# A 32-expert layer on one core: another order of the expert groups, 26 weight units, host-made layouts, and a gate that moves out of the front

## The chip, the cores and the metric

One core of a Trainium2 chip (trn2). The metric is the time of one execution on the device in microseconds (us); lower is better. Host-side preparation of the inputs is outside it. A difference is given in us or in per cent of the median before.

## The reference, cut to what matters

`x` has 256 tokens of 1024 features, `ctx` another 256. All is float32.

```python
sh1, sc1, g1, sh2, sc2, g2 = ada_params(c, ada_w, ada_b)     # silu(c) @ ada_w + ada_b, six parts of 1024
hx = modulate(x, sh1, sc1)                                    # layer norm, then *(1+sc1) + sh1
proj_x = hx @ w_in                                            # q, k, v and the 2*512 columns of the gating unit
att_x = neighbourhood_attention(q_x, k_x, v_x, k_c, v_c, rpb) # 8 heads, window and context keys in one softmax
sgu_x = spatial_gating(gelu(proj_x[..., U_OFF:]), ...)        # 128x128 mixing matrix for each of 4 groups
x = layer_norm(ALPHA * x + g1 * (concat(att_x, sgu_x) @ w_out), ln1_g, ln1_b)
h = modulate(x, sh2, sc2)
gates = softmax of the 4 largest of h @ router_w + router_b   # 32 experts
for e in range(32):                                           # w_gu: 1024x2048, w_down: 1024x1024
    gu = h @ w_gu[e] + b_gu[e]
    y += gate[e] * (((clip(gu[1024:]) + 1) * swiglu(gu[:1024])) @ w_down[e] + b_down[e])
x = layer_norm(ALPHA * x + g2 * y, ln2_g, ln2_b)
```

## The kernel before, in words

**The front** computes the adaLN vectors, the projection, attention, gating, the output projection, the first layer norm and the router. **The experts** follow: all 32 are computed, each with 12 MB of weights, cut into 12 pieces of 1 MB (8 of `w_gu`, 4 of `w_down`).

**The ring.** SBUF holds `NU` = 24 units of 8 KB per partition. `unit` takes the first of the list `free_slots`, `release` puts one at its end. Everything large lives in units: the weights of the front, working tiles, the expert pieces. The list is worked out when the program is written: a DMA into a unit waits, on the chip, for the last instruction that uses what lay there before, wherever in the program that instruction stands. `stream` is the list of all pieces in the order in which they are wanted; `pump` takes a unit and issues the next piece, `weights` hands out a piece, `done` releases its unit and pumps one more, unless that would leave fewer than `reserve[0]` free. Nearly all DMAs are issued in this one order by SyncE (SP), with eight in flight at most, and SP issues nothing past one that waits.

**The groups.** Experts are ranked by token count on the chip, so several share the 128 rows of a matmul: a *quad* is four experts of 32 rows (48 pieces), a *pair* two of 64 rows (24 pieces), a *single* one of 128 rows (12 pieces). Group 0 is the experts 0 and 1; twelve groups follow in the order of `PLAN`. Each goes through `group`: `gu_step` for gate half 0, linear half 0, gate half 1, linear half 1, each with a hook between its two halves of the contraction (`in0` to `in3`), `swiglu_gate` and `swiglu_lin` on VectorE (DVE) and ScalarE (ACT), `h_T`, then `down`, `scaled`, and the `scatter` of the group before at `gu1`.

**What the steps touch.** `front_u` is one unit for the whole front: silu(c) (`sT`, the stationary operand of every ada step), the router's weights, the ada biases. It is released (L1010) just before group 0. `ada_step` (L605) multiplies one 1 MB block of `ada_w`; the four blocks `adaG` give the second residual's gate g2. Two run as fillers of the attention, two inside `route_mm(0)` (L901), then `finish_G` (L849) spreads g2 over the partitions on GpSimd (POOL). `flip_heads` (L350) and `mask_bias` (L527) make the table of position biases on PE, ACT and POOL. `spread` (L1401) makes the rows ln2_g and ln2_b into 128 partitions. `overflow_items` (L1322) is a loop under a condition on a count, for experts with more tokens than their rows; its body does not run here, but SP waits there for every DMA in flight. `down_cols` is used in the last group only, with small last pieces (`DOWN_ROWS`).

```python
PLAN = [QUADS[0], SINGLES[0], PAIRS[0], QUADS[1], PAIRS[1], SINGLES[1], QUADS[2], PAIRS[2], PAIRS[3], QUADS[3], PAIRS[4],
        PAIRS[5]]
...
    def done(key, refill=True):
        release(loaded.pop(key)[0])
        if refill:
            pump(1, keep=reserve[0])
...
        if gi == 5:
            l2_u, row_u = unit("l2"), unit("row")
            reserve[0] = 0
            SP.dma_start(row_u[0:1, 0:D], ln2_g)
```

Of the kernel before, what the change touches and what calls it, by code (L numbers as in the profile page):

```python
# [9 lines left out]
F32 = mybir.dt.float32  # L10
# [24 lines left out]
PLAN = [QUADS[0], SINGLES[0], PAIRS[0], QUADS[1], PAIRS[1], SINGLES[1], QUADS[2], PAIRS[2], PAIRS[3], QUADS[3], PAIRS[4],  # L35
        PAIRS[5]]
DOWN_ROWS = (((0, 512), (512, 512)), ((0, 512), (512, 256), (768, 128), (896, 128)))
NU = 24


def front_blocks():
# [13 lines left out]
    for name, col in (("adaS", 4096), ("adaG", 5120)):  # L55
        out += [((name, i), "ada_w", i * 256, col, 1024) for i in range(4)]
        if name == "adaS":
            out += wo[0:2]
    return out
# [6 lines left out]
def hybrid_layer_kernel(  # L66
    ctx: ExitStack,
    tc: tile.TileContext,
    x, c, cx, c_ctx, w_front, ada_b, rpb, sgu_ln_g, sgu_ln_b, sgu_w, sgu_b,
# [8 lines left out]
    ada_b, rpb = ada_b[0], rpb[0]  # L78
    sgu_w, sgu_b = sgu_w[0], sgu_b[0]
# [105 lines left out]
    SP.dma_start(crow[0:8, :], c.rearrange("o (k p) -> (o k) p", p=P))  # L185
    SP.dma_start(crow[8:16, :], c_ctx.rearrange("(k p) -> k p", p=P))
# [12 lines left out]
    G.memset(flip, 1.0)  # L199
    G.affine_select(out=flip, in_=flip, compare_op=ALU.is_equal, fill=0.0, base=-63, pattern=[[1, 64]],  # L200
                    channel_multiplier=1)
    G.memset(bsel, 0.0)
    G.memset(bsel[:, :, 0:2], 1.0)
    G.affine_select(out=bsel, in_=bsel, compare_op=ALU.is_equal, fill=0.0, base=0,
                    pattern=[[1, 12], [0, 32]], channel_multiplier=-1)
    one_r = cst.tile([12, 1], F32, name="one_r")
    G.memset(one_r, 0.0)
    for r in (2, 3, 8, 9):
        G.affine_select(out=one_r, in_=one_r, compare_op=ALU.not_equal, fill=1.0, base=-r,
                        pattern=[[0, 1]], channel_multiplier=1)  # L210
# [8 lines left out]
    stream.extend((key, block(i, n)) for i, (key, _, _, _, n) in enumerate(FRONT))  # L219

    def group_stream(gid, ranks, by_cols=False):
# [17 lines left out]
        def col_piece(a, r0, rows, col, n):  # L239
            def fn(t):  # L240
                v = t[:, 0:rows // P * n].rearrange("p (k n) -> p k n", n=n)
                for r in range(r0, r0 + rows, 256):
                    k0, k1 = r // P % 2, min(r // P % 2 + (r0 + rows - r) // P, 2)
                    SP.dma_start(v[:, (r - r0) // P:(r - r0) // P + k1 - k0, :],  # L244
                                 expert(w_dn, a)[r // 256].rearrange("p (k n) -> p k n", k=2)[:, k0:k1, col:col + n])
                return v
            return fn
# [7 lines left out]
        if by_cols:  # L255
            for nn in range(2):
                for r0, rows in DOWN_ROWS[nn]:
                    for a in range(n):
                        stream.append(((gid, "c", nn, r0, a), col_piece(a, r0, rows, nn * 512, 512)))
        else:  # L260
            for i in range(4):
                for a in range(n):
                    stream.append(((gid, "d", i, a), piece(w_dn, a, i, 1024)))

    group_stream(0, None)

# [23 lines left out]
    T2_u = [unit("T2") for _ in range(2)]  # L290
    T2 = [u[:, 0:1536].rearrange("p (h m n) -> p h m n", h=4, m=6) for u in T2_u]
# [28 lines left out]
    def ln_transpose(t):  # L320
        for hh in range(2):
            pt = ax_bank()
            for k in range(4):
# [4 lines left out]
    pT = ax_bank()  # L328
    PE.transpose(pT[:, 0:16], crow, ident[32:48, 32:48])
    sg = front_u[:, 2016:2048].rearrange("p (a n) -> p a n", a=2)  # L330
    S.activation(sg[:, 0, :], pT[:, 0:16], AF.Exp, scale=-1.0)
# [3 lines left out]
                    pT[:, 0:16].rearrange("p (i k) -> p i k", i=2), op=ALU.mult)  # L335


    r0_ = R_u[64:128, 0:64]

    def flip_begin(h, b):  # L340
        for r2 in range(2):
            PE.matmul(b[64 * r2:64 * r2 + 64, 0:384], flip,
                      bass.AP(tensor=r0_.tensor, offset=r0_.offset + h * 250 + (1 - r2) * 31,
                              ap=[list(r0_.ap[0]), [31, 6], [1, 64]]), start=True, stop=True)
        return h, b

    def flip_end(h, b):
        S.copy(T2[h // 4][:, h % 4], b[:, 0:384].rearrange("p (m n) -> p m n", m=6))

    def flip_heads(hs):  # L350
        for h in hs:
            flip_end(*flip_begin(h, ax_bank()))
# [7 lines left out]
    flip_heads(range(0, 1))  # L360
# [3 lines left out]
    flip_heads(range(1, 2))  # L364
# [3 lines left out]
    V.tensor_scalar_add(adab, adab, one_r)  # L368
# [12 lines left out]
    ones_b = cst.tile([P, P], BF16, name="ones_b")  # L381
    G.memset(ones_b, 1.0)
# [6 lines left out]
    fold4 = cst.tile([P, NE], F32, name="fold4")  # L389
# [19 lines left out]
    def ada_quarter(q):  # L409
        bank = ax_bank()  # L410
        for j in range(4):
            row = (2 if j > 1 else 0) + q // 2
            off = (q % 2) * 256 + (j % 2) * P
            PE.matmul(bank[32 * j:32 * j + 32, 0:P], bsel[:, row, :], adab[:, off:off + P],
                      start=True, stop=False)
        for k in range(KT):
            for j in range(4):
                w = weights(("ada", j // 2, q))
                PE.matmul(bank[32 * j:32 * j + 32, 0:P], sT[:, k, :], w[:, k, (j % 2) * P:(j % 2 + 1) * P],
                          start=False, stop=k == KT - 1)  # L420
        for i in range(2):
            done(("ada", i, q))
        rows = rowsq[q % 2]
        V.tensor_copy(rows, bank[:, 0:P])
        return bank, rows
# [80 lines left out]
    fl = [flip_begin(h, ax_bank()) for h in range(2, 4)]  # L506
# [975 lines left out]
```

## Time and profile before

| what | value |
|---|---|
| runs before | 1157.69, 1158.47, 1159.37 us; median 1158.47 us |
| profiled execution | 1159.04 us, of which the span of the trace is 1157.3 us |
| PE busy, granted clock | 1011.2 us (87% of the span), mean clock 0.949 |
| DVE, ACT, POOL busy | 311.0, 137.7, 40.1 us |
| moved by DMA | 449.76 MB, mean 389 GB/s |

The trace is of one execution, 0.57 us above the median; 1.74 us of its time lie outside the span. Times in the rows are us from the span's start. A busy PE is not a PE at its peak, and the idle time of an engine costs something only where the end waits for it.

### The profile page before, as it was taken

To read this page: it belongs to the slowest core of one execution; us is meant where nothing else is said; L and a number is where in the kernel's file an instruction comes from. 1 tells how busy PE (TensorE), PEld (TensorE's weight loads), DVE (VectorE), ACT (ScalarE), POOL (GpSimd) and SP (SyncE) were. 2 spreads that over 40 slices of the span, in tenths; PEclk is the share of its full clock that TensorE was granted. 3 is DMA by queue.
4 is the path that set the end of the run, shared out by engine and by line. 5 is a ranking of instruction groups with operands and counts; after the bars stand their busy time and mean duration, and the time that the engine had idled before them with its cause. 6 is when DMAs were issued, how large, how long until landed. Compare 5 with 4: busy or idle time off the path is not lost. (4 is left out here: it accounts for less than half of the span.)

```text
span 1157.3 us, 13460 instructions
## 1 busy us (share of the span) xinstructions
PE 1011.2 (87%) x5225; PEld 427.9 (37%) x5225; DVE 311.0 (27%) x621; ACT 137.7 (12%) x297; POOL 40.1 (3%) x72
## 2 busy tenths in 40 slices
PE   6999998999779999976759999879999777689995
PEld 4798555443213534221114353213434112124221
DVE  5687756313103121210111212102121111012114
ACT  4344343110000101000001010000101000000000
POOL 3300301000000000000000000000000000000000
PEclk9999998999989999998869999989999989899998
DMA  9977789889999999999998978999999999999985
GB/s 346 372 277 290 303 305 389 301 372 426 426 428 426 427 427 426 427 426 428 427 426 351 427 262 347 425 428 427 427 426 427 427 426 427 427 426 427 426 334 206
DMA packets 68624, 449.76 MB, mean 389 GB/s; under 512 B 8495, under 2 KB 9663, under 8 KB 15565
## 3 DMA queue, kind: packets, MB, share of 16 engines
q1 hardware_dynamic: 68534, 448.85, 94.2%
q8 instruction: 42, 0.69, 0.2%
q14 instruction: 24, 0.20, 0.0%
q10 hardware_dynamic: 24, 0.02, 0.0%
HBM read 447.80 MB, written 1.05 MB: 388 GB/s over the span
## 5 line engine op out<-in xcount | busy, mean ns | idle before, releaser
L1192 PE MATMUL mm<-w,xg 128*32 128x512 f32 (+2 forms) x2048 | 419.2, 616 | 37.2 <-DMA w<-in_exp_w_gu_dram 37.1
L1236 PE MATMUL mm<-w,t 128*32 128x512 f32 (+2 forms) x960 | 226.2, 695 | 54.1 <-DMA w<-in_exp_w_down_dram 45.4
L1192 PEld LDWEIGHTS mm<-w,xg 128*32 128x32 f32 (+2 forms) x2048 | 128.2, 130 | 314.7 <-issue 236.6
L1236 PEld LDWEIGHTS mm<-w,t 128*32 128x32 f32 (+2 forms) x960 | 62.8, 140 | 205.7 <-issue 108.2
L1276 DVE TENSOR_TENSOR t<-mm,late 128x512 f32<-128x512 f32 x26 | 18.0, 692 | 271.2 <-PE mm L1236 256.3
L1215 DVE TENSOR_SCALAR t<-mm 128x512 f32<-128x512 f32 x26 | 18.0, 692 | 244.9 <-PE mm L1192 244.9
L1208 ACT ACTIVATE t<-t 128x512 f32<-128x512 f32 x26 | 16.4, 630 | 519.2 <-DVE t L1206 519.2
L1206 DVE TENSOR_SCALAR t<-mm 128x512 f32<-128x512 f32 x26 | 18.0, 691 | 201.3 <-PE mm L1192 201.3
L972 PE MATMUL mm<-bgu,sel 32*128 32x512 f32 x104 | 58.2, 639 | 1.3 <-DVEq L1324 1.3
L1259 PE MATMUL ax<-t,sT 128*128 128x512 f32 x100 | 46.2, 604 | 0.8 <-DVE t L1276 0.8
L270 POOL TENSOR_TENSOR rs<-rs,mhalf 128x1 f32<-128x1 f32 x12 | 10.0, 836 | 1056.4 <-DVE mv L282 931.6
L1227 ACT COPY t<-ax 128x512 f32<-128x512 f32 x26 | 15.0, 577 | 260.6 <-PE ax L1223 260.6
L966 PE MATMUL ax<-oh,tM 128*128 128x128 f32 x384 | 44.8, 275 | 0.0
L966 PEld LDWEIGHTS ax<-oh,tM 128*128 128x128 f32 x384 | 43.8, 192 | 0.0
L1261 DVE TENSOR_TENSOR xin<-xin,ax 128x512 f32<-128x512 f32 x50 | 33.2, 684 | 5.0 <-PE ax L1259 4.6
L467 DVE TENSOR_TENSOR wlo<-w,whi 128x1024 fp32r<-128x1024 f32 x20 | 30.1, 1540 | 3.5 <-ACT whi L464 3.5
L1259 PEld LDWEIGHTS ax<-t,sT 128*128 128x128 f32 x100 | 18.1, 189 | 28.9 <-issue 23.5
L972 PEld LDWEIGHTS mm<-bgu,sel 32*128 32x128 f32 x104 | 15.3, 183 | 31.7 <-issue 20.4
L858 ACT ACTIVATE xg<-ax,sh,sc 128x128 f32<-128x128 f32 x60 | 22.5, 459 | 32.8 <-PE ax L966 26.8
L1404 PE MATMUL ax<-row,l 1*128 1x512 f32 x8 | 5.7, 851 | 20.5 <-DMA row<-in_ln_g_dram 20.5
L464 ACT CAST whi<-w 128x1024 fp32r<-128x1024 f32 x20 | 20.1, 1049 | 9.4 <-PE mm L499 9.4
L1223 PEld LDWEIGHTS ax<-ident,t 128*128 128x128 f32 x104 | 11.2, 140 | 21.8 <-issue 18.5
(286 smaller groups left out, 788.0 us busy)
## 6 DMA issues: line engine op xcount, KB each, us to landing
w<-in_exp_w_gu_dram SPq DMA_DIRECT2D x256, 1024.0 KB, 19.4
w<-in_exp_w_down_dram SPq DMA_DIRECT2D x120, 1024.0 KB, 19.5
w<-in_w_front_dram SPq DMA_DIRECT2D x38, 1024.0 KB, 7.1
w<-in_exp_w_down_dram SPq DMA_DIRECT2D x14, 512.0 KB, 11.3
xin<-in_x_dram SPq DMA_DIRECT2D x2, 512.0 KB, 3.9
cin<-in_ctx_dram SPq DMA_DIRECT2D x2, 512.0 KB, 8.4
w<-in_exp_w_down_dram SPq DMA_DIRECT2D x4, 256.0 KB, 9.4
out_dram<-xin SPq DMA_DIRECT2D x4, 256.0 KB, 2.0
```

The costliest lines, as they stand in the source:

```text
L464: S.copy(av[:, k], w[:, k])
L467: V.tensor_tensor(bv[:, k], w[:, k], av[:, k].bitcast(F32), op=ALU.subtract)
L858: S.activation(dst[:, kk, :], src, AF.Identity, scale=sc2[:, kk:kk + 1], bias=sh2[:, kk:kk + 1])
L966: PE.matmul(bank[:, k * P:(k + 1) * P], late["tMv"][:, t, (hh * 4 + k) * P:(hh * 4 + k + 1) * P], oh[:, t].rearrange("p n w -> p (n w)"), ...
L972: PE.matmul(b, sel[r, :], bgu[r, :], start=True, stop=False)
L1192: PE.matmul(b[a * w:(a + 1) * w, :], xg[:, half * 4 + k, a * w:(a + 1) * w], weights((gid, part, j, half, a))[:, k, :], start=False, stop= ...
L1206: V.tensor_scalar_min(gtile, b, 7.0)
L1215: V.tensor_scalar(lt, b, 7.0, -7.0, op0=ALU.min, op1=ALU.max)
L1236: PE.matmul(ys[nn][a * w:(a + 1) * w, :], hTt[:, (2 * i + k) * P + a * w:(2 * i + k) * P + (a + 1) * w], weights((gid, "d", 2 * jh + i, a) ...
L1259: PE.matmul(b, st[:, t, :], ys[nn], start=True, stop=True)
L1261: V.tensor_tensor(sl, sl, b, op=ALU.add)
L1276: V.tensor_tensor(y, bank, late_v["g2"][:, nn * 512:(nn + 1) * 512], op=ALU.mult)
```

## The change

It does these things at once:

- **Order**: `PLAN` puts the second single behind the second quad, at gi 5, and a quad last. `overflow_items` moves from the last group to gi 5, with the units it needs kept free from gi 4.
- **Units**: `NU` is 26.
- **ln2 rows**: loaded by ACT at the start of gi 2 straight into `l2_u`, spread in gi 4; `row_u` is gone.
- **Gate g2**: the four `adaG` blocks leave the front. They stand in the stream after 8 and after 12 pieces of group 0; their ada steps run in group 0, at `in2` and `in3`, and `finish_G` after them. `sT` still lies in `front_u`, and `release(front_u)` still stands before group 0 (L923 of the new code).
- **Host-made layouts**: the ada biases as rows that DVE adds (the bias matmuls L414 and L609 go); the whole masked position table (two loads of 768 KB in the place of one of 500 KB; L342, L348 and L530 go); `sgu_w` transposed (L594 goes); the condition vector transposed.
- **Down**: `w_down` is laid out by column halves, and every group runs `down` half by half; the last group's small pieces are contiguous.

```diff
-PLAN = [QUADS[0], SINGLES[0], PAIRS[0], QUADS[1], PAIRS[1], SINGLES[1], QUADS[2], PAIRS[2], PAIRS[3], QUADS[3], PAIRS[4],
-        PAIRS[5]]
+PLAN = [QUADS[0], SINGLES[0], PAIRS[0], QUADS[1], SINGLES[1], PAIRS[1], PAIRS[2], QUADS[2], PAIRS[3], PAIRS[4],
+        PAIRS[5], QUADS[3]]
-NU = 24
+NU = 26
...
-    S.dma_start(adab, ada_b.rearrange("(r n) -> r n", n=512))
+    S.dma_start(arow, ada_rows[:, 0:768])
...
     stream.extend((key, block(i, n)) for i, (key, _, _, _, n) in enumerate(FRONT))
+    gate_blocks = [stream.pop() for _ in range(4)][::-1]
...
     group_stream(0, None)
+    at = len(stream) - 24 + 8
+    stream[at:at] = gate_blocks[0:2]
+    stream[at + 6:at + 6] = gate_blocks[2:4]
...
+    T2_u = [unit("T2") for _ in range(2)]
+    T2 = [u[:, 0:1536].rearrange("p (h m n) -> p h m n", h=4, m=6) for u in T2_u]
+    for u in range(2):
+        SP.dma_start(T2_u[u][:, 0:1536], rpb[u])
...
-        6: [lambda: ada_step("adaG", 10, 0), lambda: ada_step("adaG", 10, 1)],
...
     def finish_G():
+        rows = t2("rows")
+        V.tensor_tensor(rows[:, 0:256], ada_bank["adaG"][:, 0:256], late_v["bdn"], op=ALU.add)
         for j in range(4):
-            G.partition_broadcast(late_v["g2"][:, j * 256:(j + 1) * 256], late["rows"][32 * j:32 * j + 1, :])
+            G.partition_broadcast(late_v["g2"][:, j * 256:(j + 1) * 256], rows[32 * j:32 * j + 1, 0:256])
+        for r in range(4):
+            S.dma_start(late_v["bdn"][r * NE:(r + 1) * NE, :], b_dn[:, r * 256:(r + 1) * 256])
...
-        if t == 0:
-            for i in range(2):
-                part_mm(range(4 * i, 4 * i + 1))
-                ada_step("adaG", 10, 2 + i, lambda: part_mm(range(4 * i + 1, 4 * i + 3)))
-                part_mm(range(4 * i + 3, 4 * i + 4))
-        else:
-            part_mm(range(KT))
+        part_mm(range(KT))
...
         if gi == 0:
             hooks["in0"] += [rank_counts]
             hooks["gu0"] += [rank_order, streams]
-            hooks["gu1"] += [finish_G]
+            hooks["in2"] += [lambda: ada_step("adaG", 0), lambda: ada_step("adaG", 1)]
+            hooks["in3"] += [lambda: ada_step("adaG", 2), lambda: ada_step("adaG", 3), finish_G]
...
         if gi == 2:
-            ovf_u = unit("ovf")
+            ovf_u, l2_u = unit("ovf"), unit("l2")
...
+            S.dma_start(l2_u[0:1, 0:D], ln2_g)
+            S.dma_start(l2_u[0:1, D:2 * D], ln2_b)
...
-        if gi == 5:
-            l2_u, row_u = unit("l2"), unit("row")
-            reserve[0] = 0
-            SP.dma_start(row_u[0:1, 0:D], ln2_g)
-            SP.dma_start(row_u[0:1, D:2 * D], ln2_b)
...
             hooks["in1"] += [lambda: spread((0, 1))]
             hooks["in2"] += [lambda: spread((2, 3))]
...
             reserve[0] = 4
-        if gi == len(groups) - 1:
+        if gi == 5:
             pending()
             hooks["gu1"].remove(pending)
             overflow_items()
```

**SP, at the end of the front**: the third to the seventh `w_down` piece of group 0, before. In brackets is what a DMA waits for on the chip; `DMAHW` is its lane, one of eight, held by the DMA issued eight earlier.

```order
L235 DMA w_1870<-in_exp_w_down_dram 128x2048 [waits DMAHW5_49,DVE_49]
L235 DMA w_1872<-in_exp_w_down_dram 128x2048 [waits DMAHW6_49,Activation_49]
L235 DMA w_1874<-in_exp_w_down_dram 128x2048 [waits DMAHW7_49,DVE_49]
L235 DMA w_1916<-in_exp_w_down_dram 128x2048 [waits DMAHW0_49,PE_49]
L235 DMA w_1922<-in_exp_w_down_dram 128x2048 [waits DMAHW1_49,PE_49]
```

And now:

```order
L223 DMA w_1733<-in_exp_w_down_dram 128x2048 [waits DMAHW3_49,DVE_49]
L223 DMA w_1735<-in_exp_w_down_dram 128x2048 [waits DMAHW4_49,Activation_49]
L223 DMA w_1737<-in_exp_w_down_dram 128x2048 [waits DMAHW5_49,DVE_49,PE_49]
L223 DMA w_1779<-in_exp_w_down_dram 128x2048 [waits DMAHW6_49]
L223 DMA w_1785<-in_exp_w_down_dram 128x2048 [waits DMAHW7_49]
L223 DMA w_1806<-in_exp_w_down_dram 128x2048 [waits DMAHW0_49]
L987 DMA late_1808<-in_ada_rows_dram 128x256 [waits DMAHW1_49]
```

`w_1874` and `w_1737` are the pieces that take the unit of `front_u`. The first waits for DVE alone (the last use there was a step of the routing); the second waits for DVE and for a count of PE. Before it stand now two pieces of `w_down` in the place of four.

**PE, the last uses of `front_u`** (`front_84`), before, inside `route_mm(0)`, where L616 is the ada step:

```order
L907 MATMUL ax_1744<-xg_1567,front_84 32x128
L616 MATMUL ax_1494<-w_1202,front_84 32x256 x4
L907 MATMUL ax_1744<-xg_1567,front_84 32x128 x2
L616 MATMUL ax_1494<-w_1202,front_84 32x256 x4
L907 MATMUL ax_1744<-xg_1567,front_84 32x128 x2
L616 MATMUL ax_1494<-w_1303,front_84 32x256 x4
```

And now, between the two halves of the last `gu_step` of group 0 (L1104 is `gu_step`, L537 the ada step):

```order
L1104 MATMUL mm_1989<-w_1570,xg_1452 64x512
L1104 MATMUL mm_1989<-w_1572,xg_1452 64x512
L537 MATMUL ax_1917<-w_1486,front_84 32x256 x8
L537 MATMUL ax_1917<-w_1568,front_84 32x256 x8
L1104 MATMUL mm_1989<-w_1607,xg_1452 64x512
L1104 MATMUL mm_1989<-w_1609,xg_1452 64x512
```

The matmuls that read `sT` from `front_84` last have moved from the router into group 0. The row with `w_1568` is the one whose count `w_1737` waits for.

## Rows read from the trace of the kernel before

**Rows 1.** The page: GB/s in 40 slices; queue: packets, MB, share of 16 engines.
```profile
GB/s 346 372 277 290 303 305 389 301 372 426 426 428 426 427 427 426 427 426 428 427 426 351 427 262 347 425 428 427 427 426 427 427 426 427 427 426 427 426 334 206
...
q1 hardware_dynamic: 68534, 448.85, 94.2%
```

**Rows 2.** Windows of four stages: busy by engine, clock, DMA share, GB/s.
```profile
0.00:250.00 250.00, 231.15 (x1588) 153.40 (x1590) 151.62 (x305) 87.45 (x189) 38.89 (x70) 0.97 0.84 324
575.00:600.00 25.00, 8.27 (x16) 2.63 (x18) 0.00 (x0) 1.17 (x2) 0.00 (x0) 0.50 1.01 427
600.00:725.00 125.00, 123.54 (x540) 49.68 (x540) 27.50 (x52) 9.35 (x20) 0.00 (x0) 0.99 0.89 352
1100.00:1157.00 57.00, 42.58 (x168) 13.26 (x162) 15.79 (x26) 1.69 (x3) 1.22 (x2) 0.95 0.70 270
```

**Rows 3.** Timeline, PE, 10 to 40 us: start, duration, instructions [idle before].
```profile
12.11 1.55 PE L342 MATMUL ax<-R,front 64*64 64x384 f32 x4
...
34.26 0.42 PE L414 MATMUL ax<-front 12*32 12x128 f32 x8
...
38.12 0.33 PE L430 MATMUL ax<-ident,front 128*128 128x128 f32 x1 [1.55 <-DVE front L424]
```

**Rows 4.** Groups of instructions by line, 28 to 40 us.
```profile
L467 DVE TENSOR_TENSOR wlo<-w,whi 128x1024 fp32r<-128x1024 f32 x3 | 10.0, 3352 | 0.1
L530 POOL TENSOR_TENSOR T<-T,front 128x1536 f32<-128x1536 f32 x2 | 8.5, 4276 | 4.8 <-ACT T L348 4.8
L342 PE MATMUL ax<-R,front 64*64 64x384 f32 x16 | 2.8, 487 | 0.0
```

**Rows 5.** Timeline, PE, 71 to 162 us.
```profile
71.32 0.60 PE L594 MATMUL ax<-ident,t 128*128 128x128 f32 x4
...
158.65 0.63 PE L609 MATMUL ax<-front 12*32 12x256 f32 x8
159.22 1.93 PE L616 MATMUL ax<-w,front 128*32 128x256 f32 x32
```

**Rows 6.** Waits of the DMA queue, SP, 196 to 250 us: total, times, longest.
```profile
SPq L235 <- DVE oh L953: 10.7, 1, 10.7
```

**Rows 7.** Timeline, SP, 201 to 242 us.
```profile
201.44 0.33 SPq L235 DMA_DIRECT2D w<-in_exp_w_down_dram  x1
...
218.89 13.36 SPq L235 DMA_DIRECT2D w<-in_exp_w_gu_dram  x7
...
240.93 0.91 SPq L235 DMA_DIRECT2D w<-in_exp_w_gu_dram  x2
```

**Rows 8.** Timeline, PE, first expert pair, 205 to 244 us.
```profile
205.27 5.51 PE L1192 MATMUL mm<-w,xg 128*64 128x512 f32 x16
...
237.25 7.09 PE L1192 MATMUL mm<-w,xg 128*64 128x512 f32 x32
```

**Rows 9.** Window of 4 us around the last pause of the transfers.
```profile
240.00:244.00 4.00, 4.00 (x22) 1.32 (x20) 0.00 (x0) 0.00 (x0) 0.00 (x0) 1.00 0.39 152
```

**Rows 10.** Timeline, PE, 591 to 700 us.
```profile
591.73 3.75 PE L1404 MATMUL ax<-row,l 1*128 1x512 f32 x4 [20.48 <-DMA row<-in_ln_g_dram]
595.40 6.63 PE L1192 MATMUL mm<-w,xg 128*64 128x512 f32 x16
...
606.65 3.65 PE L1192 MATMUL mm<-w,xg 128*64 128x512 f32 x16
...
643.44 1.12 PE L972 MATMUL mm<-bgu,sel 32*128 32x512 f32 x2
...
698.73 1.12 PE L972 MATMUL mm<-bgu,sel 32*128 32x512 f32 x2
```

**Rows 11.** Waits of the DMA queue, SP, 1085 to 1120 us.
```profile
SPq L1324 <- SPq L1324: 19.1, 8, 3.6
```

**Rows 12.** The chain that ended last: start, duration, what.
```profile
1137.23 7.07 PE mm L1249 x32
```

**Rows 13.** Window of 4 us around the last landing.
```profile
1140.00:1144.00 4.00, 4.00 (x20) 1.15 (x16) 0.00 (x0) 0.00 (x0) 0.00 (x0) 1.00 0.13 49
```

More of the change, by code (lines that the diff above doesn't have):

```diff
@@ L54, in front_blocks @@
     out += wo[2:4]
[L55 to L59, printed above, removed]
+    out += [(("adaS", i), "ada_w", i * 256, 4096, 1024) for i in range(4)] + wo[0:2]
+    return out + [(("adaG", i), "ada_w", i * 256, 5120, 1024) for i in range(4)]
 FRONT = front_blocks()
@@ L237, in piece, with col_piece @@
             return fn
-        def col_piece(a, r0, rows, col, n):
+        def col_piece(a, r0, rows, nn):
             def fn(t):
[L241 to L246, printed above, removed]
+                k = rows // P
+                SP.dma_start(t[:, 0:k * 512], expert(w_dn, a)[2 * nn + r0 // 512][:, r0 % 512 * 4:r0 % 512 * 4 + k * 512])
+                return t[:, 0:k * 512].rearrange("p (k n) -> p k n", n=512)
             return fn
@@ L254, in group_stream @@
                                        piece(w_gu, a, part * 4 + j * 2 + half, 512)))
[L255 to L259, printed above, removed]
-        else:
-            for i in range(4):
+        for nn in range(2):
+            for r0, rows in DOWN_ROWS[nn if last else 0]:
                 for a in range(n):
-                    stream.append(((gid, "d", i, a), piece(w_dn, a, i, 1024)))
+                    stream.append(((gid, nn, r0, a), col_piece(a, r0, rows, nn)))
     group_stream(0, None)
+    at = len(stream) - 24 + 8
+    stream[at:at] = gate_blocks[0:2]
+    stream[at + 6:at + 6] = gate_blocks[2:4]
     def rsqrt(var):
@@ L334, in hybrid_layer_kernel @@
     V.tensor_tensor(sT[:, :, 0:2].rearrange("p k i -> p i k"), sg[:, 1, :].rearrange("p (i k) -> p i k", i=2),
[L335 to L352, printed above, removed]
+                    cT.rearrange("p (i k) -> p i k", i=2), op=ALU.mult)
     ln_head(0)
@@ L603, in hybrid_layer_kernel, with ada_step @@
     ada_bank = {}
-    def ada_step(name, row, i, between=None):
+    def ada_step(name, i, between=None):
         if i == 0:
             ada_bank[name] = ax_bank()
-            for j in range(4):
-                PE.matmul(ada_bank[name][32 * j:32 * j + 32, 0:256], bsel[:, row + j // 2, :],
-                          adab[:, (j % 2) * 256:(j % 2) * 256 + 256], start=True, stop=False)
         w = weights((name, i))
@@ L1455, in _laid_out @@
     a["w_front"] = np.stack(blocks)
+    a["cond"] = np.stack([a["c"][0].reshape(KT, P), a["c_ctx"].reshape(KT, P)]).transpose(2, 0, 1).reshape(P, 2 * KT)
+    rows = np.zeros((P, 1024), np.float32)
+    bias = a["ada_b"][0]
+    for j in range(4):
+        for r in (32 * j, 32 * j + 1):
+            for q in range(4):
+                at = j // 2 * D + q * 256 + j % 2 * P
+                rows[r, q * P:(q + 1) * P] = bias[at:at + P]
+            for i in range(2):
+                at = (4 + i) * D + j * 256
+                rows[r, 512 + i * 256:768 + i * 256] = bias[at:at + 256]
+    a["ada_rows"] = rows
+    a["sgu_w"] = a["sgu_w"][0].transpose(2, 0, 1).reshape(P, 512)
+    col, key = np.arange(64)[:, None], np.arange(64)[None, :]
+    start = np.clip(col - 8, 0, 48)
+    seen = (key >= start) & (key < start + 16)
+    dc = np.where(seen, key - col + 15, 0)
+    table = np.full((H, 2, 64, 6, 64), NEG, np.float32)
+    for r in range(2):
+        for m in range(6):
+            table[:, r, :, m, :] = np.where(seen, a["rpb"][0][:, m + 5 - r][:, dc], NEG)
+    a["rpb"] = table.reshape(2, 4, 2, 64, 6, 64).transpose(0, 2, 3, 1, 4, 5).reshape(2, P, 1536)
     a["exp_w_gu"] = a["exp_w_gu"][0].reshape(NE, 2, 4, P, 2, 2, 512).transpose(0, 4, 5, 1, 3, 2, 6).reshape(NE, 8, P, 2048)
-    a["exp_w_down"] = a["exp_w_down"][0].reshape(NE, 4, 2, P, D).transpose(0, 1, 3, 2, 4).reshape(NE, 4, P, 2048)
+    a["exp_w_down"] = a["exp_w_down"][0].reshape(NE, 2, 4, P, 2, 512).transpose(0, 4, 1, 3, 2, 5).reshape(NE, 4, P, 2048)
     return a
```

161 lines of the change are left out of this document (49 added, 112 removed).

## The prediction

> **What bounds the kernel now.** I read the page first. Its row of GB/s shows a kernel that streams weights: in most slices the rate stands at 426 to 428, and the one queue moves 448.85 MB [rows 1]. At 427 GB/s that takes 1051 us, so of 1157 us some 106 are time in which the queue moved less than it could. Windows over the span say where [rows 2]: 250 x (1 - 324/427) = 60 us in the front, 125 x (1 - 352/427) = 22 us between 600 and 725, 57 x (1 - 270/427) = 21 us at the end. So the end is set by the transfers, and PE counts only where it leaves the queue without a free unit or comes last after the last landing. One piece of 1 MB (1.049 MB) costs 2.456 us at that rate. I cost the change in these three places and look in each for what the queue waits for.
>
> **Front, first step: group 0 starts earlier.** The first expert matmul starts at 205.27. What leaves PE's path before it:
> - Eight flip matmuls in two sets of 1.55 us before 16 us [rows 3]. PE has idle time there, so I take 1.5 of 3.1 us (0 to 3.1).
> - Between 28 and 40 us: 2.8 us of flips on PE; and DVE's L467 takes 3352 ns a time, 10.0 us for three, while POOL runs L530 for 8.5 us [rows 4]. Of L467's slowness PE shows 1.55 us as an idle gap at 38.12 [rows 3]. The sum is 4.35; I take 4 (3 to 6; the upper end is where DVE's delay also held up work that I can't single out).
> - Bias matmuls: 0.42 us per ada quarter [rows 3], two quarters counted: 0.8. The transposes of the mixing matrix 0.6, the bias of adaG 0.63, and two ada steps 1.93 [rows 5]. The other two adaG steps stood in the routing, which DVE sets; nothing for them.
>
> That is 1.5 + 4 + 0.8 + 0.6 + 2.56 = 9.5, of which I take 9 (6.5 to 11): group 0 starts at T = 196.3. DVE adds the biases now in the instruction that copied before, and the wider table is loaded behind the projection: nothing.
>
> **Front, second step: the queue is stopped.** A unit is given out when the program is written, but the DMA into it waits on the chip for the unit's last reader. Before, the fifth `w_down` piece went into the unit of `front_u`, whose last reader on its way was a DVE step of the routing; that is SP's longest single wait near there, 10.7 us [rows 6], and the piece went out at 201.44 [rows 7]. Now `sT` in the same unit is read by the last adaG step, in the middle of group 0's last `gu_step`. The third `w_down` piece takes this unit and waits for that matmul, and SP issues in order, so the other five, the row of biases and all pieces of the later groups stand behind it.
>
> When is it released? The last `gu_step` starts 237.25 - 205.27 = 31.98 us after the first and its 7.09 us are 32 matmuls, so its first half ends 35.5 us after T [rows 8]. Four ada steps now lie before that, 2 x 1.93 [rows 5]: 39.4 us. From issue to flowing data: SP's last long wait before ended with the issue at 240.93 [rows 7], and the window 240 to 244 moved at 152 GB/s, which is 1.4 us at full rate [rows 9], so data flowed from 242.6, some 1.7 us later. Now: T + 41.1 = 237.4 us, against 242.6 before.
>
> What is left to move at that moment differs. Before, seven pieces of group 1 were out before 240.93 [rows 7] and all of group 0. Now none of group 1's and six of group 0's `w_down` are still to come, with the small bias rows: 13.3 pieces x 2.456 = 32.7 us. Afterwards 26 units, of which 16 were emptied by then, keep the queue full as before. **Term 1: 237.4 + 32.7 - 242.6 = +27.5 us** (24.5 to 29.5, from T and half a piece).
>
> Behind this stop, PE waits for the `w_down` pieces, finish_G's DVE addition waits for the bias rows, and the clip of the linear half waits behind that addition on DVE; all of it ends before the second group's weights are there, so it adds nothing. The new loads on ACT's queue share lanes with SP, and come while SP is stopped.
>
> **Middle.** PE stands idle 20.48 us until 591.73 for the row of ln2_g, which SP issued behind eight pieces of the stream; then sixteen matmuls take 6.63 us, and the same work at 606.65 takes 3.65 [rows 10]. The granted clock in that stretch was 0.50 [rows 2], the lower level (1.2 of 2.4 GHz). Pair and single follow, and PE needs 698.73 - 643.44 = 55.3 us for the single [rows 10], whose 12 pieces come in 29.5: the ring fills, and the queue loses its 22 us [rows 2]. Now the rows are loaded two groups ahead of their use, so this idle time goes. The single comes behind a quad, in which transfers (118 us) are far longer than PE's work, so PE enters it waiting for data. It falls 55.3 - 29.5 = 26 us behind, plus some 5 that I estimate it to lag anyway: 31. Of 26 units some 8 hold other things or are kept free, so the ring covers 18 x 2.456 = 44 us: no loss. The pairs behind it (59 us of transfers each) don't add. **Term 2: -22 us** (-22 to -14, the upper end if a third of the filling stays).
>
> The overflow loop's branch makes SP wait for all eight transfers in flight: 19.1 us in eight waits [rows 11]. It moves to gi 5 with the same wait, most of which the transfers in flight fill. What it costs is paid there as it was paid in the last group: zero difference.
>
> **Tail.** Before, the last column half's 32 matmuls ran from 1137.23 to 1144.30 [rows 12]; 49 GB/s in 1140 to 1144 is 0.2 MB [rows 13], so the last landing was near 1140.5, and PE came 3.8 us after it. In a quad the transfers of a half (8 MB, 19.7 us) are longer than its matmuls, and after the last landing stand one row of four matmuls of 0.22 us: 0.9. The 2 KB rows of the column pieces become contiguous: 0 to 1 us. **Term 3: -3.5 us** (-4.5 to -1). A rule of the Trainium skill ("DMA: Bandwidth & Descriptors", section "Bandwidth") wants 1 MiB at least for most of the peak, and the last pieces of the quad are of 256 KB; by it the gain of the contiguous rows would be eaten again, and the sum would be 1 us higher. No run here shows such pieces alone.
>
> **The sum**: 27.5 - 22 - 3.5 = +2.0 on the profiled execution's 1159.04, 1161.0. That execution lies 0.57 above the median of 1158.47, so I forecast **1160.5 us**. Two large terms of opposite sign almost cancel. By the bounds of the terms: 24.5 - 22 - 4.5 = -2 to 29.5 - 14 - 1 = +14.5, so 1156.5 to 1173.
>
> **The rivals.**
> - *The stop costs little (faster).* If the count that the piece waits for is reached with the routing, as before, the queue goes on at T with everything: term 1 becomes -9 (T) + 2.5 (1 MB more of position table) = -6.5, and the sum -32: about **1126.5**. For it speaks that before the same unit was free at 201.44 [rows 7]; against it that PE's row stands where it stands. It also decides in part if the piece waits for less than the last step: each 2.456 us of earlier release give a piece back. Chance 0.13.
> - *The stop costs less than a pure shift (faster).* In the front's last stretch the queue before loses time to free units, too; if the first term is only 18 to 22 us (say, if T falls to 190 or the restart finds pieces already out), the sum is -4 to -8: about **1153**. Chance 0.15.
> - *The single fills the ring (slower).* PE's granted clock was 0.50 from 575 to 600, in the idle stretch [rows 2], and a set of sixteen then took 6.63 in the place of 3.65 us [rows 10]. If PE enters the single at the lower level and stays there, the single takes 55.3 x 6.63 / 3.65 = 100 us, PE falls 31 + 45 = 76 us behind, 32 more than the ring covers, and the sum is +34: **1192.5**. It decides from 44 us of lag on; 13 us of slow matmuls more than forecast are still covered. A third of it (or a ring that is smaller by five units) gives **1172**. For it: PE waits much in the quads ahead. Against: sixteen took 3.65 us again 11 us later [rows 10]. The Trainium skill ("TensorE: Matmul & The Clock Gate", section "HAM oscillation — how this bites in real kernels") says that waits for data between bursts of matmuls throttle the engine again and again; by it a starved quad would hand PE over slow, and this case would be the likeliest. The trace agrees that idle time lowers the clock, and speaks against its lasting in a single, whose data lie ready. Chance 0.14.
>
> **How the numbers follow.** The forecast's case has 0.58; a measurement of this kernel can tell some 0.2% (2.3 us) from no change. Within the case, the sum lies between -2 and +14.5 with the most likely at +2: faster by over 2.3 us 0.08, within 0.17, slower 0.33. With the rivals: faster 0.08 + 0.13 + 0.15 = 0.36, same 0.17, slower 0.33 + 0.14 = 0.47. The range leaves out the first rival and the far end of the third, and takes in the second and the third's mild end: 1150 to 1174; the likeliest case's own is 1156.5 to 1173.
>
> **What would show it.** In the changed profile: the first expert matmul at 196 us (194 to 199); SP's longest wait, near 30 us, ahead of the third `w_down` piece, released by the ada step at L537; the rate at zero for some 30 us up to 237 us; no idle PE for a row of ln2; 427 GB/s from the restart to the branch, and after it through the single; the last matmul within 1.5 us of the last landing. Wrong it would be if the rate never falls to zero near 235 us (first rival), or if it dips again behind gi 5 (third).

## The result and the profile after

The changed kernel takes **1178.13 us** (median of 4 runs, 1175.67 to 1179.24) against 1158.36 us before (4 runs): ratio 1.0167, 95% interval 1.0148 to 1.0186. It is 19.8 us slower. The forecast was 1160.5 us with a range of 1150 to 1174: the sign of the largest chance was right, the time lies 4 us outside the range.

The page of the changed kernel, GB/s in 40 slices of 29.4 us and the queue, answers to [rows 1]:

```profile
GB/s 384 419 402 302 227 315 181 1 375 421 421 422 421 422 422 421 421 421 421 421 420 346 421 422 421 420 422 421 421 421 421 421 421 421 421 421 422 421 420 196
...
q1 hardware_dynamic: 65890, 449.90, 93.0%
```

Two things stand there. The eighth slice is at 1: the queue stood still, as forecast. And no slice in the saturated part is above 422, where 426 to 428 stood before. Windows show both (columns as in [rows 2]; last GB/s):

```profile
175.00:200.00 25.00, 21.20 (x108) 13.37 (x107) 14.78 (x48) 7.30 (x21) 2.01 (x2) 0.80 0.57 235
200.00:225.00 25.00, 25.00 (x141) 8.76 (x137) 7.67 (x26) 2.48 (x5) 0.00 (x0) 1.00 0.00 1
236.00:240.00 4.00, 4.00 (x23) 1.35 (x21) 0.00 (x0) 0.00 (x0) 0.00 (x0) 1.00 0.70 238
260.00:600.00 340.00, 289.16 (x1372) 98.77 (x1369) 59.09 (x126) 18.72 (x40) 0.00 (x0) 0.94 1.01 421
620.00:630.00 10.00, 10.00 (x52) 6.58 (x51) 2.75 (x6) 2.56 (x7) 0.00 (x0) 1.00 0.54 193
660.00:1140.00 480.00, 420.76 (x1982) 145.54 (x1980) 78.93 (x150) 26.88 (x58) 0.00 (x0) 0.97 1.01 421
```

Before, two windows of the same kind:

```profile
260.00:590.00 330.00, 274.87 (x1375) 95.72 (x1373) 58.25 (x129) 16.99 (x37) 0.00 (x0) 0.93 1.01 427
720.00:1090.00 370.00, 316.43 (x1512) 108.46 (x1506) 55.45 (x106) 19.82 (x44) 0.00 (x0) 0.94 1.01 427
```

The stop itself, in the waits of SP from 180 to 260 us (total, times, longest):

```profile
SPq L223 <- PE ax L537: 43.3, 1, 43.3
SPq L223 <- DVE pm L863: 10.4, 1, 10.4
```

And PE in group 0:

```profile
196.73 5.42 PE L1104 MATMUL mm<-w,xg 128*64 128x512 f32 x16
...
234.22 1.93 PE L537 MATMUL ax<-w,front 128*32 128x256 f32 x32
...
239.57 3.60 PE L1150 MATMUL mm<-w,t 128*64 128x512 f32 x16
251.94 1.11 PE L1135 MATMUL ax<-ident,t 128*128 128x128 f32 x4 [8.77 <-DVE t L1128]
...
275.49 3.62 PE L1104 MATMUL mm<-w,xg 128*32 128x512 f32 x26 [1.44 <-DMA w<-in_exp_w_gu_dram]
```

Group 0 starts at 196.73 (forecast 196.3). SP waits 43.3 us for the ada step at L537, the second pair of which ends at 236.1. The forecast had this wait near 30 us; its sum goes by the end of the wait, not by its length. In 236 to 240 the rate is 238, which is 2.3 us at 421, so data flow from 237.7 (forecast 237.4). PE then stands 8.77 us for DVE's clip, as the chain behind the bias rows was told. The queue loses nothing by it that the windows show (421 from 260 on), and PE waits for weights again at 275.49. From 260 to 1140 the rate is level but for one dip of 5 us at 620 to 630, the overflow branch in its new place; no dip comes behind the single at gi 5.

The end, three windows and the last down matmuls of the last quad:

```profile
1150.00:1154.00 4.00, 3.44 (x33) 0.96 (x30) 1.47 (x3) 0.00 (x0) 0.00 (x0) 1.00 1.01 368
1154.00:1158.00 4.00, 3.64 (x22) 0.77 (x16) 0.00 (x0) 0.00 (x0) 0.00 (x0) 1.00 0.91 316
1158.00:1162.00 4.00, 4.00 (x16) 0.82 (x12) 0.00 (x0) 0.00 (x0) 0.00 (x0) 1.00 0.34 92
```

```profile
1156.18 6.22 PE L1150 MATMUL mm<-w,t 128*32 128x512 f32 x26 [0.19 <-DMA w<-in_exp_w_down_dram]
```

Before, the column pieces moved at 406 GB/s from 1124 to 1140. Now the last pieces come at 368, then at 316, and the last bytes trickle in until between 1160 and 1161; PE ends its down matmuls at 1162.40.

### The profile page after: what moved, and what is told of

It is laid out like the page before. It is cut to its first block, busy times and chain, and to the rows that moved or that the text cites. A ratio compares the mean times of both kernels' runs of the same rounds, so it can differ in the third digit from the quotient of the medians.

```text
span 1175.5 us, 13238 instructions
## 1 busy us (share of the span) xinstructions
PE 1020.8 (87%) x5140; PEld 427.9 (36%) x5140; DVE 305.8 (26%) x621; ACT 133.1 (11%) x286; POOL 28.5 (2%) x57
## 2 busy tenths in 40 slices
DMA packets 66296, 451.32 MB, mean 384 GB/s; under 512 B 8627, under 2 KB 8883, under 8 KB 12725
## 5 line engine op out<-in xcount | busy, mean ns | idle before, releaser
L1104 PE MATMUL mm<-w,xg 128*32 128x512 f32 (+2 forms) x2048 | 440.0, 633 | 53.2 <-DMA w<-in_exp_w_gu_dram 53.0
L1150 PE MATMUL mm<-w,t 128*32 128x512 f32 (+2 forms) x1024 | 237.5, 655 | 54.4 <-DMA w<-in_exp_w_down_dram 45.7
L1104 PEld LDWEIGHTS mm<-w,xg 128*32 128x32 f32 (+2 forms) x2048 | 130.9, 132 | 346.8 <-issue 239.9
L1150 PEld LDWEIGHTS mm<-w,t 128*32 128x32 f32 (+2 forms) x1024 | 67.4, 135 | 212.5 <-issue 111.6
L886 PEld LDWEIGHTS mm<-bgu,sel 32*128 32x128 f32 x104 | 15.3, 183 | 34.5 <-issue 25.5
L1135 PE MATMUL ax<-ident,t 128*128 128x128 f32 x104 | 17.3, 290 | 10.3 <-DVE t L1128 10.3
L415 DVE TENSOR_TENSOR wlo<-w,whi 128x1024 fp32r<-128x1024 f32 x20 | 23.7, 1225 | 3.1 <-ACT whi L412 3.1
L1135 PEld LDWEIGHTS ax<-ident,t 128*128 128x128 f32 x104 | 11.5, 143 | 30.9 <-issue 16.0
## 6 DMA issues: line engine op xcount, KB each, us to landing
w<-in_exp_w_gu_dram SPq DMA_DIRECT2D x256, 1024.0 KB, 19.8
w<-in_exp_w_down_dram SPq DMA_DIRECT2D x124, 1024.0 KB, 19.8
```

Of the source, the lines that this page charges most:

```text
L415: V.tensor_tensor(bv[:, k], w[:, k], av[:, k].bitcast(F32), op=ALU.subtract)
L886: PE.matmul(b, sel[r, :], bgu[r, :], start=True, stop=False)
L1104: PE.matmul(b[a * w:(a + 1) * w, :], xg[:, half * 4 + k, a * w:(a + 1) * w], weights((gid, part, j, half, a))[:, k, :], start=False, stop= ...
L1135: PE.transpose(b[:, k * P:(k + 1) * P], lt[:, k * P:(k + 1) * P], ident)
L1150: PE.matmul(bank[a * w:(a + 1) * w, :], hs[kk // 4][:, kk % 4 * P + a * w:kk % 4 * P + (a + 1) * w], weights((gid, nn, r0, a))[:, k, :], s ...
```

## The experiments

Each time is the median of its runs; ratios are to the kernel before on the same chip.

**What lowers the rate: where the units start.** At the start of a partition the program lays a descriptor scratch (a reserve whose size is set when the program is built), then the constants, then the units. Before, the scratch takes 16384 bytes and the first unit starts at byte 26368, which is 103 x 256. The change has three more edits, which the cut of the diff under "The change" does not show:

```diff
-    ones_b = cst.tile([P, P], BF16, name="ones_b")
-    G.memset(ones_b, 1.0)
+    one_b = cst.tile([P, 1], BF16, name="one_b")
+    G.memset(one_b, 1.0)
+    ones_b = one_b.to_broadcast([P, P])
...
-    fold4 = cst.tile([P, NE], F32, name="fold4")
+    fold4 = front_u[:, 2016:2048]
...
-    nc = _bacc.Bacc("TRN2", target_bir_lowering=False, num_devices=1)
+    nc = _bacc.Bacc("TRN2", target_bir_lowering=False, num_devices=1, dynamic_dma_scratch_size=256)
```

The first unit now starts at 9888, which is 38 x 256 + 160. The scratch is 16128 bytes smaller, which is 63 x 256 and leaves the offset as it was. The two constants give up 352 bytes (tiles are laid in steps of 32 bytes, so `ones_b` goes from 256 to 32, and the 128 of `fold4` go), and these move it. Each unit is 8192 bytes, so all 26 share the offset. Four kernels tell the place from its rivals.

*a_256*, the changed kernel with units at a multiple of 256:

```diff
-    one_b = cst.tile([P, 1], BF16, name="one_b")
+    one_b = cst.tile([P, 49], BF16, name="one_b")
-    ones_b = one_b.to_broadcast([P, P])
+    ones_b = one_b[:, 0:1].to_broadcast([P, P])
```

> The changed kernel with one constant tile 96 bytes wider, so that each of the 26 weight units starts at a multiple of 256 bytes in its partition (now 160 bytes past one; the kernel before: at a multiple). Theory (the rate fell from 427 to 421 GB/s because of where the units start): the rate in the saturated stretches is 427 again, and some 920 us of stream after the stop at group 0 take 13 us less: about 1165 us. Rival (the rate fell because of the 26 units, the small descriptor scratch, or the new layout of the down weights): 421 GB/s stays, 1177 to 1179 us.

Measured: 1165.43 us, ratio 1.0069 (1.0051 to 1.0087). The window 260 to 590:

```profile
260.00:590.00 330.00, 284.04 (x1367) 97.72 (x1363) 58.86 (x125) 18.69 (x40) 0.00 (x0) 0.95 1.01 427
```

*a_64*: the same tile with 17 columns, so that units start at 9920 = 64 x 155, 192 past a multiple of 256.

> The changed kernel with the same tile 32 bytes wider: units start at a multiple of 64 bytes, 192 past a multiple of 256. If a multiple of 64 is enough for the full rate: 427 GB/s and about 1165 us. If it takes a multiple of 256: 421 GB/s and 1177 to 1179 us. Anything between the two rates would say that the price grows with the distance.

Measured: 1177.36 us, ratio 1.0156 (1.0130 to 1.0182):

```profile
260.00:590.00 330.00, 281.93 (x1357) 96.55 (x1355) 56.13 (x121) 18.67 (x40) 0.00 (x0) 0.95 1.01 421
```

*b_off*: the kernel before, with 96 bytes less of scratch; units start at 26272, 160 past a multiple of 256.

```diff
-    nc = _bacc.Bacc("TRN2", target_bir_lowering=False, num_devices=1)
+    nc = _bacc.Bacc("TRN2", target_bir_lowering=False, num_devices=1, dynamic_dma_scratch_size=16288)
```

> The kernel before with 96 bytes less of descriptor scratch at the start of the partition, nothing else: units start 160 bytes past a multiple of 256, as in the changed kernel. Theory: 421 GB/s in place of 427 in the saturated stretches, 1.4% of some 850 us at full rate: about 12 us slower, 1170. Rival (the place does not matter): 1158.

Measured: 1167.98 us, ratio 1.0086 (1.0069 to 1.0103):

```profile
260.00:590.00 330.00, 279.32 (x1387) 97.13 (x1382) 59.26 (x130) 16.99 (x37) 0.00 (x0) 0.94 1.01 421
```

*b_scr*: the kernel before with the scratch of the change (`dynamic_dma_scratch_size=256`); units start at 10240 = 20 x 512.

> The kernel before with a descriptor scratch of 256 bytes as in the changed kernel; its units then start at a multiple of 512. Theory (only the place matters): 427 GB/s, 1158 us. Rival (the small scratch slows the transfers): 421 GB/s, about 1170 us. A rate above 427 would say that a multiple of 512 is better still than 256.

Measured: 1155.59 us, ratio 0.9986 (0.9971 to 1.0000):

```profile
260.00:590.00 330.00, 270.52 (x1366) 96.64 (x1358) 57.88 (x128) 16.96 (x37) 0.00 (x0) 0.94 1.01 427
```

What follows: a multiple of 256 gives 427, an offset of 160 or of 192 gives 421, in either kernel, with 24 units or 26, with either scratch and either layout of the down weights. So the place alone sets the rate, and it is worth 1.0167 - 1.0069 = 1.0% or some 11 us here. The Trainium skill ("DMA: Bandwidth & Descriptors", section "How a descriptor splits into AXI transactions") says, of reading, that a descriptor which doesn't start at a multiple of 256 bytes begins with a transaction from the boundary below, of which part is unused. The trace agrees in the direction, here for rows that are written. By that page's count an 8 KB row that starts 160 past a boundary takes 261 beats in place of 256, an estimate of 2.0%, and one that starts 192 past it 262, an estimate of 2.3%; measured are 427/421 = 1.4% for both, and the measurement decides. By what mechanism the offset costs this, no run here shows.

**What the stop costs.** *a_keep256* is a_256 with the front's unit released inside group 0:

```diff
-    release(front_u)
     pump(NU)
...
-            hooks["in3"] += [lambda: ada_step("adaG", 2), lambda: ada_step("adaG", 3), finish_G]
+            hooks["in3"] += [lambda: ada_step("adaG", 2), lambda: ada_step("adaG", 3), finish_G,
+                             lambda: release(front_u), lambda: pump(NU)]
```

> a_256 with the unit of the front (which holds silu(c)) released behind the last ada step of the gate, inside group 0, not before group 0; the third down piece then takes another unit. Theory (that wait of SP, 43 us long, costs 34 us against a front without it: +27.5 forecast, -6.5 without): 34 us less than a_256, about 1131 us, and no stretch of zero GB/s near 200 to 237. Rival (the queue would have stood still there anyway, for free units): less than 15 us gained, 1150 or more.

Measured: 1134.77 us, ratio 0.9808 (0.9787 to 0.9830), 30.7 us less than a_256 and faster than both kernels of this case. The 43 us wait is gone, and the stretch that stood at 1 GB/s moves at 363. SP's waits from 175 to 250, and three windows:

```profile
SPq L223 <- PE mm L1103: 22.9, 3, 15.7
SPq L216 <- DMA late<-in_exp_b_down_dram: 11.5, 1, 11.5
```

```profile
200.00:225.00 25.00, 25.00 (x160) 11.52 (x156) 7.53 (x18) 3.49 (x6) 0.00 (x0) 1.00 0.95 363
230.00:235.00 5.00, 5.00 (x50) 1.88 (x42) 0.42 (x1) 0.00 (x0) 1.80 (x4) 1.00 0.27 99
235.00:240.00 5.00, 4.32 (x24) 1.56 (x22) 1.38 (x2) 0.58 (x1) 0.00 (x0) 1.00 0.77 298
```

Of the 34 us expected 30.7 came. SP has a new wait in there, 11.5 us for one of the four small loads of the down biases on ACT's queue: that load waits for the DVE addition of the gate's bias, which reads the buffer that the load overwrites and ends at 232.06, and SP's next piece shares its lane and goes out at 235.16. The rate falls to 99 and 298 for it.

*k_lane* takes these loads away from ACT's queue: the gate's bias row goes into free columns of the front's unit.

```diff
         SP.dma_start(l1[:, 1, :], row_bc(ln1_b, D))
+        SP.dma_start(front_u[:, 1632:1888], ada_rows[:, 768:1024])
...
-    V.tensor_tensor(rows[:, 0:256], ada_bank["adaG"][:, 0:256], late_v["bdn"], op=ALU.add)
+    V.tensor_tensor(rows[:, 0:256], ada_bank["adaG"][:, 0:256], front_u[:, 1632:1888], op=ALU.add)
...
-        for r in range(4):
-            S.dma_start(late_v["bdn"][r * NE:(r + 1) * NE, :], b_dn[:, r * 256:(r + 1) * 256])
...
-        SP.dma_start(late_v["bdn"], ada_rows[:, 768:1024])
+        for r in range(4):
+            SP.dma_start(late_v["bdn"][r * NE:(r + 1) * NE, :], b_dn[:, r * 256:(r + 1) * 256])
```

> a_keep256 with the gate's bias row loaded in the front (into the front's unit) and the down biases loaded by SP as in the kernel before; the four loads on ACT's queue behind the gate's broadcast are gone. In a_keep256 SP waits 11.5 us for one of these four loads, whose lane its next piece shares, and the rate falls to 99 and 298 GB/s in two windows of 5 us. Theory (this wait costs what the rate shows, 5 us): about 1130 us, no wait of SP for the down biases. Rival (the queue has as much in flight that it does not matter): the same as a_keep256, 1135.

Measured: 1132.97 us, ratio 0.9791 (0.9774 to 0.9808). SP's waits and a window:

```profile
SPq L223 <- PE mm L1103: 21.5, 3, 15.7
SPq L216 <- PE mm L1103: 13.6, 4, 8.5
```

```profile
225.00:235.00 10.00, 10.00 (x74) 4.28 (x74) 1.28 (x4) 1.76 (x5) 1.41 (x4) 1.00 0.94 377
```

The lane's wait is gone and the rate from 225 to 235 is 377. But the intervals of the two kernels overlap, so a gain is not shown; part of the time comes back as waits for free units (13.6 us, which did not stand there so long before).

**What the middle is worth.** *b_l2* is the kernel before with the loads of the ln2 rows one group earlier, in the old order:

```diff
-        if gi == 4:
+        if gi == 3:
             reserve[0] = 2
-        if gi == 5:
+        if gi == 4:
             l2_u, row_u = unit("l2"), unit("row")
...
             V.memset(l2_u[0:1, 2 * D - P:2 * D], 1.0)
-
+        if gi == 5:
             def spread(js):
```

> The kernel before with the two loads of the ln2 rows put one group earlier (gi 4 in place of gi 5) and the units for them kept free from gi 3; the order of the groups stays. Theory (the 22 us lost between 600 and 725 us come from PE's idle wait for these rows, which the single behind it then turns into a full ring): the wait goes and 427 GB/s goes through, 20 to 22 us less: about 1136 us. Rival (the single fills the ring in any case, and the new order is what helps): less than 8 us gained, 1149 or more.

Measured: 1137.52 us, ratio 0.9828 (0.9809 to 0.9848), 19.9 us less (1.72%). PE goes through without the 20.48 us gap of [rows 10], and the stretch that lost 22 us runs at the full rate:

```profile
566.28 3.75 PE L1192 MATMUL mm<-w,xg 128*64 128x512 f32 x16
569.96 1.98 PE L1404 MATMUL ax<-row,l 1*128 1x512 f32 x4
571.87 3.65 PE L1192 MATMUL mm<-w,xg 128*64 128x512 f32 x16
```

```profile
600.00:675.00 75.00, 73.54 (x250) 31.38 (x248) 14.52 (x27) 4.67 (x10) 0.00 (x0) 1.00 1.01 427
675.00:1000.00 325.00, 271.54 (x1364) 89.50 (x1360) 45.80 (x90) 16.33 (x36) 0.00 (x0) 0.94 1.01 427
```

*k_oldplan* is a_keep256 with the order of the groups of before (the `PLAN` of the diff, turned back).

> a_keep256 with the order of the groups of the kernel before (second single at gi 6 behind a pair, a pair last); the overflow branch stays at gi 5, the ln2 rows stay early. Theory (the order as such is worth nothing once the ln2 wait is gone, since the ring covers a single's lag of about 31 us): the same as a_keep256 within 3 us. Rival (the order carries the gain of the middle): 10 us or more slower, with a dip of the rate behind the single.

Measured: 1140.35 us, ratio 0.9851 (0.9835 to 0.9868), 5.6 us more than a_keep256: more than expected from no difference, less than the rival. The window with the branch, and the single behind it:

```profile
580.00:620.00 40.00, 39.27 (x196) 15.42 (x192) 6.21 (x11) 3.45 (x8) 0.00 (x0) 1.00 0.92 379
620.00:700.00 80.00, 79.27 (x332) 32.80 (x332) 18.74 (x37) 4.71 (x10) 0.00 (x0) 1.00 1.01 427
```

There is no dip behind the single, which is what the rival needed. So the middle's 20 us are the ln2 loads' and not the order's. The two profiled executions differ by 6.6 us. Some 3 of these lie in the front (331 against 336 GB/s over 250 us), where both kernels run the same instructions; they are put down to the execution, which is not shown. The rest is the end, since here a pair ends the kernel: from 1100 us to the end of the span the queue loses 37.3 x (1 - 210/427) = 19.0 us, in a_keep256 30.7 x (1 - 213/427) = 15.4.

*k_nu24* is k_lane with `NU = 24`.

> k_lane with 24 units in place of 26, their places unchanged. Theory (with transfers as the bound the ring only has to cover a single's lag of some 31 us): the same within 2 us, up to 5 us more where the end of the front waits for units. Rival (two units fewer let the single fill the ring): 10 us or more slower, with a dip of the rate behind the second single.

Measured: 1137.18 us, ratio 0.9819 (0.9800 to 0.9837), 4 us more than k_lane; the intervals overlap. Behind the branch nothing dips:

```profile
600.00:1090.00 490.00, 440.10 (x2031) 153.78 (x2029) 81.66 (x154) 27.40 (x59) 0.00 (x0) 0.97 1.01 427
```

The two units do not decide in the middle; whether they are worth something in the front stays open.

**What the tail is worth.** *k_rows* is a_keep256 with `DOWN_ROWS` of 512 rows throughout.

> a_keep256 with the last group's pieces all of 512 rows, as in the other groups. Theory (the small last pieces, whose rows in a partition are 2 KB, slow the last 2 MB, 334 and 182 GB/s in two windows of 4 us): the last landing comes some 2 us earlier and the end 0 to 2 us earlier. Rival (small pieces let PE end sooner behind the last landing): 1 to 3 us slower, since 16 matmuls wait for each of the last landings.

Measured: 1137.02 us, ratio 0.9808 (0.9788 to 0.9829), the ratio of a_keep256 to the fourth digit (by the medians 2.3 us more). Large pieces hold the full rate longer, but not to the end:

```profile
1112.00:1116.00 4.00, 3.16 (x28) 0.84 (x20) 0.00 (x0) 0.00 (x0) 0.00 (x0) 1.00 1.01 426
1116.00:1120.00 4.00, 2.09 (x4) 0.28 (x4) 0.00 (x0) 0.00 (x0) 0.00 (x0) 1.00 0.66 281
```

From 1100 to its end this execution loses 38.0 x (1 - 238/427) = 16.8 us, 1.4 more than a_keep256's 15.4. That is the rival's direction; the times do not tell the two apart.

*k_pair* is k_lane with the last two groups exchanged, so that a pair comes last.

> k_lane with the last two groups exchanged, so that a pair ends the kernel and not a quad. Theory (behind a pair PE ends some 7 us after the last landing, behind a quad 2 us, but the quad's small pieces slow the last transfers by some 3 us): 2 to 5 us slower than k_lane. Rival (the last group is worth nothing): within 1 us of k_lane.

Measured: 1134.44 us, ratio 0.9816 (0.9796 to 0.9836), 1.5 us over k_lane by the medians and 0.25% by the ratios, with intervals that overlap. Its last down matmuls and the window of the last landing:

```profile
1110.66 7.09 PE L1149 MATMUL mm<-w,t 128*64 128x512 f32 x32
```

```profile
1112.00:1116.00 4.00, 4.00 (x22) 1.43 (x20) 0.64 (x1) 0.00 (x0) 0.00 (x0) 1.00 0.03 9
```

The last landing is between 1112 and 1113, and PE ends at 1117.75, some 5 us behind it; in the changed kernel, with the quad, it ends some 2 us behind. From 1100 to the end of the span, k_pair and then k_lane:

```profile
1100.00:1131.10 31.10, 18.66 (x76) 6.19 (x76) 11.86 (x21) 0.59 (x1) 1.22 (x2) 0.91 0.42 168
```

```profile
1100.00:1129.20 29.20, 16.38 (x73) 4.12 (x72) 11.63 (x20) 0.00 (x0) 1.22 (x2) 0.88 0.53 202
```

The pair's tail loses 31.1 x (1 - 168/427) = 18.9 us, the quad's 29.2 x (1 - 202/427) = 15.4. So the quad saves 3.5 us in the tail, as the theory had it, though the times of the two kernels do not show it clear of noise. k_oldplan (pair, 19.0) and a_keep256 (quad, 15.4) say the same.

## Why the prediction was wrong

**The rate was taken as a constant, and that is the step that failed.** The prediction priced every piece behind the stop at 2.456 us, "at that rate" of 427, and said that the ring would "keep the queue full as before". It was full, but at 421 GB/s: 2.49 us a piece. Over the 920 us from the restart to the end that is 13 us, and putting the units back gave 12.7 by the medians of the changed kernel and a_256, 11.3 by the ratios. The cause stands in the change, in lines that neither the list nor the cut of the diff under "The change" shows and that the prediction passed over: two constants became narrower, and that moved the place of every unit. No rival held it.

**Where the rest of the time went.** a_256 streams at 427 as the kernel before does, so the two can be compared without the place. A stretch loses its length times (1 - rate/427). Three windows of the kernel before, with one of the branch in its last group, and three of a_256:

```profile
0.00:260.00 260.00, 240.48 (x1629) 156.47 (x1630) 152.62 (x307) 88.03 (x190) 38.89 (x70) 0.97 0.84 328
590.00:725.00 135.00, 131.81 (x554) 52.32 (x558) 27.50 (x52) 10.52 (x22) 0.00 (x0) 0.96 0.90 358
1100.00:1157.30 57.30, 42.58 (x168) 13.26 (x162) 15.79 (x26) 1.69 (x3) 1.22 (x2) 0.94 0.69 269
1104.00:1116.00 12.00, 12.00 (x49) 4.00 (x50) 1.90 (x3) 1.10 (x2) 0.00 (x0) 1.00 0.62 243
```

```profile
0.00:260.00 260.00, 229.74 (x1519) 152.24 (x1521) 147.13 (x307) 83.28 (x179) 27.32 (x55) 0.94 0.73 288
590.00:725.00 135.00, 132.02 (x484) 52.98 (x486) 27.31 (x55) 8.81 (x19) 0.00 (x0) 0.97 0.98 411
1100.00:1162.80 62.80, 38.60 (x182) 9.00 (x174) 13.02 (x22) 0.59 (x1) 1.22 (x2) 0.86 0.79 320
```

| us | before | a_256 | difference |
|---|---|---|---|
| all bytes at 427 GB/s (449.76 and 451.32 MB) | 1053.3 | 1057.0 | +3.7 |
| lost in the front | 60.3 | 84.6 | +24.3 |
| lost in the middle | 21.8 | 5.1 | -16.7 |
| lost in the tail | 21.2 | 15.7 | -5.5 |
| sum | 1156.6 | 1162.4 | +5.8 |
| span | 1157.3 | 1162.8 | +5.5 |

**Term 1, the stop: right.** The releaser, the restart at 237.7 and the chain behind it came as forecast. The front's 24.3 us and the 3.7 us for more bytes make 28.0, where 27.5 was forecast. That group 0 started within 0.5 us of the forecast is luck in part: the same front starts it at 192.15 and at 198.54 in two other traces. Taking the stop away gave 30.7 us, where the forecast said 27.5 + 6.5 = 34.

**Term 2, the middle: right.** -22 was forecast, b_l2 measured -19.9; the ring covered the single's lag in either order. The rival of the filled ring did not come: the granted clock stood at 1.00 in 620 to 630 and at 0.97 on average behind it. The rule of the Trainium skill on waits between bursts ("TensorE: Matmul & The Clock Gate", section "HAM oscillation — how this bites in real kernels"), which the prediction set beside this rival, did not decide here.

**Term 3, the tail, and the branch: the quad right, the branch wrong.** The prediction gave -3.5 to the tail and said of the branch "zero difference". The quad's 3.5 us are there (k_pair against k_lane). But of the 21.2 us before, 12 x (1 - 243/427) = 5.2 were the branch, and a_256 pays 5.1 in the middle for it, so middle and tail together gained 22.2 us (0.4 beyond the 21.8 of the ln2 wait) where 25.5 were forecast. What fell short is the branch's price in its old place: a tail with a pair and the branch lost 21.2 before, a tail with a pair and no branch loses 18.9 (k_pair). So its leaving gave back some 2.3 us, and it costs 5.1 at gi 5. The layout of the last pieces differs between these two kernels as well, and no run moves the branch alone, so this split is argued and not shown. A likely reason is that PE, while the queue stood, worked off its lag: it ended 2 to 3 us behind the last landing before (windows of 1 us show bytes until after 1141, where the prediction had 1140.5), and some 5 us behind in k_pair. The rule of the Trainium skill that the prediction set beside this term ("DMA: Bandwidth & Descriptors", section "Bandwidth") fits the windows at 368 and 316, but with 1 MB pieces to the end k_rows was not faster, so no run shows that the size of the last pieces costs time.

**The sum.** Without the place the change costs 5.5 us in the profiled executions and 8.0 by the ratio of a_256 (1.0069; 6 to 10 by its interval), where +2.0 was forecast; a_256, at 1165.4 us, lies within the range. The place adds 11 to 13. Together that is 17 to 21 us, and 19.8 were measured.

None of the three rivals came. The place of the range was wrong for the same reason as the point: all its bounds were made at one rate.

## What to carry to other kernels

In a kernel that is bound by transfers, look at where the destination tiles start: a pool's base is the sum of everything laid before it, so the width of one constant can move all its tiles. Here starts at multiples of 256 bytes had the full rate, and starts at multiples of 32 and of 64 that are not multiples of 256 had not; a multiple of 128 was not tried. A buffer that is given back early in the program but read late stops the whole queue behind the DMA that takes it: move the release with the last reader. When a change has several parts, price each on its own; here the change with the units' place and the release mended (a_keep256, k_lane) is about 2% faster than before, and as it stood it was 1.7% slower. Nearly all of the 2% is one part: moving only the ln2 loads in the kernel before (b_l2) gives 1.7%.

## What the runs showed of the hardware

- The saturated rate depends on the place of an 8 KB row in a partition: 427 GB/s at multiples of 256 and of 512 bytes, 421 at 160 and 192 past a multiple of 256, in six kernels.
- A small DMA on another engine's queue that waits to be issued holds its lane: in a_keep256 SP waited 11.5 us for one of 32 KB on ACT's queue, and in k_lane, without it, that wait is gone.
- The rate falls as the last pieces come in: in the last three windows of 4 us it was 368, 316 and 92 GB/s in the changed kernel, whose pieces get smaller there, down to 256 KB, and 426, 281 and 14 in k_rows, whose pieces stay at 1 MB.
- The time of the front differs between executions of the same instructions: group 0 starts at 192.15 us in a_keep256, at 198.54 us in k_rows, whose edits differ in the last group only.
